# Sixteen weight tiles a layer split into high and low parts by two GpSimd DMAs instead of by ScalarE and VectorE

## The chip, the cores and the metric

The program runs on one core of a Trainium2 chip. The metric is the time of one execution on the device in microseconds, the median of several runs. The five engines of the core have their own instruction queues, each worked off in order: TensorE (PE, with its weight loads as PEld), VectorE (DVE), ScalarE (ACT), GpSimd (POOL) and SyncE (SP, which here only issues DMAs).

## The reference

Two layers act on `x` (512 positions, 1024 columns, float32). The part that matters here is the first third of each layer, the mixer:

```python
h = rms_norm(x, g_mix[l])
z = h @ w_in[l]                                  # 1024 -> 2560 columns
q, k, v, xb, gb = z[...]                         # 512 columns each
q = partial_rope(q, cos, sin); k = partial_rope(k, cos, sin)
o = diff_attention(q, k, v, lam)                 # 4 heads, two softmaxes each
c = centred_dwconv(xb, lru_conv_w[l], lru_conv_b[l])
h_f = rg_lru(c, ..., False); h_b = rg_lru(c, ..., True)   # sigmoid gates, exp, sqrt, scan
r = rms_norm((h_f + h_b) * jax.nn.gelu(gb), lru_norm_g[l])
x = x + jnp.concatenate([o, r], axis=-1) @ w_out[l]
```

After it come a cross-attention into 256 memory tokens and a squared-ReLU MLP, then the next layer, and a final norm.

## The kernel before

Every product is made of three TensorE passes in `float32r`: a float32 operand is split into a high part (rounded to float32r) and a low part (the rest), and the product is high by high, high by low and low by high. Activations are kept transposed, 128 rows of columns by 512 positions. Weights come from HBM as tiles of 128x1024 float32 (512 KB), 126 a layer (`NT`). Tile names in the profile: `wraw` is a weight tile as loaded, `whi` and `wlo` are its two parts, `b` are 62 buffers of 128x512, `mm` and `at` are PSUM banks, `pt` holds transposed probabilities, `s` small columns.

`weight(l, t)` delivers a tile. It takes a `wraw` buffer (3 exist), loads it from SP's queue, has ACT write `whi` and DVE write `wlo` (`split`), and the consumer `gemm_fm` uses it in 24 matmuls of 512 columns. `whi` and `wlo` have 3 buffers each (`NW`), so the buffers that tile number n takes are free only when PE has finished with tile n-3. The sixteen tiles from `T_FM` on are the columns of q and k (8 tiles, `qk_one`), of `xb` (4, `lru_conv`) and of `gb` (4, `lru_branch`), all of the mixer. The tiles of v (`T_V`), of the gates (`T_G`), and everything behind the mixer are not among them.

The program is recorded first and then ordered by a planner (`Plan`). Each recorded operation has a key, the PE time recorded so far less a lead (`plan.ahead`); `schedule` plays the engines through with cost estimates and always places the operation that can start first on its engine, the lowest key first. Loads of `wraw` lead by 65 (`LOAD_AHEAD`), splits by 12 (`SPLIT_AHEAD`). An activation whose function is not in the table that ACT holds is set back by `SWITCH`, since ACT must load a table first. Engines then run the emitted order, each in its own queue.

In the mixer, heads of attention (16 units of a score, softmax, transpose and value product) are mixed with filler pieces in the order of `ORDER`: conv tiles (X, Y), gates (P, R: 8 matmul groups each with a sigmoid on ACT, then exponentials, tanh), scans (p, r: square roots on ACT, scans on DVE), gelu tiles (B), q and k of the next heads (1, 2, 3), then the norm (N) and the memory's keys and values (K). The functions of sigmoid, exp, sqrt and gelu lie in different tables. The line of every row is L412 of the kernel before and L416 of the changed one: the loop in `emit` that issues all recorded calls.

Of the kernel before, what the change touches and what calls it, by code (L numbers as in the profile page):

```python
# [12 lines left out]
F32R = mybir.dt.float32r  # L13
I32 = mybir.dt.int32
AF = mybir.ActivationFunctionType
ALU = mybir.AluOpType
AX = mybir.AxisListType

P = 128
# [8 lines left out]
T_FM = 0  # L28
# [9 lines left out]
NT = 126  # L38
# [10 lines left out]
ATT_AHEAD = 3  # L49
SPLIT_AHEAD = 12.0  # L50
LOAD_AHEAD = 65.0


PC = {}
# [96 lines left out]
class Plan:  # L151
# [43 lines left out]
    def cost(self, eng, m, a, k):  # L195
        out = a[0] if a else k["out"]
        n = 1
        for d in out.shape[1:]:
            n *= d
        if eng == "pe":  # L200
            if m == "transpose":
                return 0.109
            f32 = a[1].root.dtype == F32
            if n < 64:
                return 0.224
            return n * 0.00176 if f32 else max(0.114, n * 0.000456)
        if m == "dma_start":
            return 0.06
        if eng == "act":
            t = 0.093 + n * 0.000833  # L210
            t += 0.093 * sum(isinstance(k.get(x), _View) for x in ("scale", "bias", "accum_out"))
            return t
        if eng == "dve":
            if m == "tensor_reduce":
                n = 512
            if m == "tensor_scalar_mul":
                return 0.066 + n * 0.0007
            ap = m == "scalar_tensor_tensor" and isinstance(a[2], _View)
            return 0.067 + n * 0.00105 + 0.06 * ap
        if eng == "pool":  # L220
            return 0.1 + n * (0.0022 if m != "memset" else 0.001)
        return 0.06

    def record(self, eng, m, a, k):
        allv = [v for v in (*a, *k.values()) if isinstance(v, _View)]
        out = [v for v in (a[0] if a else k["out"], k.get("accum_out")) if isinstance(v, _View)]
        op = self.cur
        if not isinstance(op, _Op):
            op = _Op()
            op.eng, op.calls, op.dur, op.idx = eng, [], 0.0, len(self.ops)  # L230
            op.succ, op.roots, op.new, op.ready, op.preds, op.behind = {}, [], [], 0.0, set(), set()
            op.table, op.bytes = None, 0
            op.key = self.t - self.lead
            self.ops.append(op)
            if self.cur == "open":
                self.cur = op
        assert op.eng == eng
        op.calls.append((m, a, k))
        c = self.cost(eng, m, a, k)
        op.dur += c  # L240
        if eng == "pe":
            self.t += c
        if m == "dma_start":
            v = out[0] if out else k["in_"]
            op.bytes = 4
            for d in v.shape:
                op.bytes *= d
        if m == "activation":
            op.table = self.SETS.get(str(a[2]).split(".")[-1])
        for v in allv:  # L250
            w = any(v is o for o in out)
            r, b = v.root, v.box
            if w and eng == "pe":
                b = [0, r.shape[0], 0, r.shape[1]]
            if r not in op.roots:
                op.roots.append(r)
                r.left += 1
                if not r.log:
                    op.new.append(r)
                    r.first = op  # L260
                else:
                    op.behind.add(r.first)
            for o, ob, ow in r.log:
                if o is not op and (w or ow) and b[0] < ob[1] and ob[0] < b[1] and b[2] < ob[3] and ob[2] < b[3]:
                    op.preds.add(o)
            if w and b[0] <= 0 and b[2] <= 0 and b[1] >= r.shape[0] and b[3] >= r.shape[1]:
                r.log = [e for e in r.log if e[0] is op]
            r.log.append((op, b, w))
# [146 lines left out]
def trunk(tc, ctx, xT, memT, pos, W, par, outT):  # L415
# [4 lines left out]
    plan = Plan(nc, {  # L420
        "const": (cst, 0),
        "b": (sb, NB), "xb": (sb, 2), "rb": (sb, 1), "Cr": (sb, 1), "Sr": (sb, 1),
        "wraw": (sb, NRAW), "whi": (sb, NW), "wlo": (sb, NW), "pt": (sb, 4), "s": (sb, NSM),
        "mm": (ps, NMM), "at": (ps, 8 - NMM),
    })
    V, A, G, PE, SP = (plan.engine(e) for e in ("dve", "act", "pool", "pe", "sp"))
# [19 lines left out]
    def b(v):  # L446
        return v.bitcast(F32)


    def split(dst_hi, dst_lo, src):  # L450
        A.activation(dst_hi, src, AF.Copy)
        V.tensor_tensor(dst_lo, src, b(dst_hi), op=ALU.subtract)
# [7 lines left out]
    def raw_weight(l, t, ahead=None):  # L460
        raw = plan.tile("wraw", [P, 1024], F32)
        if ahead:
            for h in range(2):
                cs = slice(h * 512, h * 512 + 512)
                with plan.ahead(ahead[h]):
                    SP.dma_start(out=raw[:, cs], in_=W[l * NT + t][:, cs])
        else:
            with plan.ahead(LOAD_AHEAD):
                SP.dma_start(out=raw, in_=W[l * NT + t])
        return raw  # L470

    def weight(l, t):
        raw = pre.pop(t, None) if l == 0 else None
        first = raw is not None
        if raw is None:
            raw = raw_weight(l, t)
        hi = plan.tile("whi", [P, 1024], F32R)
        lo = plan.tile("wlo", [P, 1024], F32R)
        with plan.ahead(SPLIT_AHEAD):
            for cs in (slice(0, 512), slice(512, 1024)) if first else (slice(0, 1024),):  # L480
                split(hi[:, cs], lo[:, cs], raw[:, cs])
        return hi, lo

    def gemm_fm(l, t, xs, out, order=range(KD)):

        hi, lo = weight(l, t)
        for i, k in enumerate(order):
            xh, xl = xs[k]
            wh = hi[:, k * P:(k + 1) * P]
            with plan.group():  # L490
                PE.matmul(out, wh, xh, start=(i == 0), stop=False)
                PE.matmul(out, wh, xl, start=False, stop=False)
                PE.matmul(out, lo[:, k * P:(k + 1) * P], xh, start=False, stop=(i == KD - 1))
# [182 lines left out]
    def v_products(l, xget):  # L676
        pms = [MM(), MM(), AT(), AT()]
        for t in range(4):
            hi, lo = weight(l, T_V + t)
            for k2 in range(2):  # L680
                k = 2 * t + k2
                xh, xl = xget(k)
                wh = hi[:, k2 * S:(k2 + 1) * S]
                wl = lo[:, k2 * S:(k2 + 1) * S]
                for c in range(4):
                    a_ = xh[:, c * P:(c + 1) * P]
                    with plan.group():
                        PE.matmul(pms[c], a_, wh, start=(k == 0), stop=False)
                        PE.matmul(pms[c], a_, wl, start=False, stop=False)
                        PE.matmul(pms[c], xl[:, c * P:(c + 1) * P], wh, start=False, stop=(k == 7))  # L690
        return pms
# [25 lines left out]
    def lru_gates(l, pr, conv, neg, posi):  # L717

        gh, gl = weight(l, T_G + pr)
        gs = {}  # L720
        for c2 in range(2):
# [311 lines left out]
    def mem_load():  # L1033
        out = []
        for i in range(2):
            m = plan.tile("wraw", [P, 1024], F32)
            with plan.ahead(LOAD_AHEAD):
                SP.dma_start(out=m, in_=memT[:, 1024 * i:1024 * (i + 1)])
# [404 lines left out]
```

## Time and profile before

| | |
|---|---|
| median of 3 runs | 1533.76 us (1530.17 to 1539.23) |
| the profiled execution's own time | 1536.88 us |
| its span | 1535.1 us |
| PE, PEld busy | 1476.1, 1242.4 us |
| DVE, ACT busy | 1183.5, 727.1 us |
| POOL busy | 54.1 us |
| TensorE's mean granted clock | 0.978 |

The span is the time between the first and last instruction of one execution. Busy time of an engine is not the time that it sets the pace; that is read from the waits.

### The profile page before, as it was taken

The page shows a single profiled execution, that of the slowest core. Times are in us where ns is not written, and L with a number is a line of the kernel's source. Part 1 is how long each engine was busy: PE and PEld are TensorE (multiplying, and loading weights), DVE is VectorE, ACT ScalarE, POOL GpSimd, SP SyncE. Part 2 cuts the span into 40 slices and gives each one's busy share as a digit, 9 for nine tenths or more (in the row PEclk, how much of TensorE's full clock was granted, in tenths as well). Part 3 has the DMA queues.
Part 4 walks back from the last instruction along what each step waited for, and adds up shares of the span by engine and source line. Part 5 has one row for each costly group of instructions (what it writes and reads, how often), then busy time and mean ns, then how long its engine had stood idle before and what let it go on. Part 6 is the DMA issues. An engine that isn't in the chain of part 4 may idle for free.

```text
span 1535.1 us, 20895 instructions
## 1 busy us (share of the span) xinstructions
PE 1476.1 (96%) x8038; PEld 1242.4 (81%) x8038; DVE 1183.5 (77%) x2107; ACT 727.1 (47%) x1099; POOL 54.1 (4%) x59
## 2 busy tenths in 40 slices
PE   8979999999999999999999799999999999999996
PEld 6757788888889889898977577888888898988985
DVE  7899886655589696979868876865656887969696
ACT  5587664444334343434535875553443433434243
POOL 0031000000000000000001310000000000000000
PEclk9989999999999999999999987999999999999998
DMA  5322342311222323222242213422112323232321
GB/s 194 97 82 78 129 138 82 110 69 56 96 96 83 110 84 122 98 97 97 87 134 81 85 57 110 144 101 96 55 69 82 110 84 107 86 110 83 116 88 58
DMA packets 45107, 148.24 MB, mean 97 GB/s; under 512 B 5584, under 2 KB 5712, under 8 KB 45008
## 3 DMA queue, kind: packets, MB, share of 16 engines
q1 hardware_dynamic: 44864, 146.65, 28.0%
q8 instruction: 63, 1.03, 0.3%
q14 instruction: 36, 0.29, 0.1%
q10 hardware_dynamic: 144, 0.26, 0.0%
HBM read 136.41 MB, written 2.10 MB: 90 GB/s over the span
## 4 chain that ended last, share of the span: by engine, by line
PE 85%; DVE 10%; issue 2%; DMA 1%; ACT 1%; SPq 0%; DVEq 0%; ACTq 0%
PE mm L412 65%; PE at L412 20%; DVE b L412 6%; DVE wlo L412 2%; DVE pt L412 1%; DVE s L412 1%; ACT b L412 1%; DMA b<-b 0%; DVE c_x L412 0%; DMA wraw<-in_W 0%; DMA c_x<-in_xT 0%; DMA wraw<-in_memT 0%; SPq L412 0%; ACT whi L412 0%; ACT Cr L412 0%
## 5 line engine op out<-in xcount | busy, mean ns | idle before, releaser
L412 PE MATMUL mm<-b,whi 128*128 128x512 f32 (+1 forms) x3648 | 991.3, 359 | 13.0 <-ACT b L412 6.2
L412 PEld LDWEIGHTS mm<-b,whi 128*128 128x128 f32 x3648 | 638.5, 190 | 126.3 <-ACT b L412 8.6
L412 PE MATMUL mm<-b,wlo 128*128 128x512 f32 (+1 forms) x1824 | 651.0, 357 | 8.0 <-DVE wlo L412 8.0
L412 ACT ACTIVATE whi<-wraw 128x1024 fp32r<-128x1024 f32 (+1 forms) x223 | 233.7, 1049 | 372.6 <-issue 168.3
L412 PEld LDWEIGHTS mm<-b,wlo 128*128 128x128 f32 x1824 | 345.8, 190 | 64.7 <-DVE wlo L412 10.0
L412 DVE TENSOR_TENSOR wlo<-wraw,whi 128x1024 fp32r<-128x1024 f32 (+1 forms) x223 | 277.1, 1243 | 37.2 <-ACT whi L412 36.9
L412 DVE TENSOR_TENSOR b<-b,b 128x512 fp32r<-128x512 f32 (+3 forms) x374 | 219.2, 602 | 15.6 <-ACT b L412 13.3
L412 ACT ACTIVATE b<-b 128x256 fp32r<-128x256 f32 (+2 forms) x224 | 130.3, 596 | 151.9 <-DVE b L412 151.3
L412 DVE TENSOR_TENSOR c_x<-c_x,mm 128x256 f32<-128x256 f32 (+1 forms) x160 | 73.8, 472 | 73.0 <-PE mm L412 71.6
L412 ACT ACTIVATE whi<-pt 128x1024 fp32r<-128x1024 f32 x64 | 67.9, 1061 | 101.6 <-PE mm L412 75.5
L412 PE MATMUL at<-b,whi 128*128 128x256 f32 x512 | 91.8, 278 | 0.0
L412 DVE TENSOR_TENSOR b<-mm,rb 128x512 f32<-128x512 f32 x72 | 49.5, 687 | 53.2 <-PE mm L412 52.5
L412 PE MATMUL at<-b,b 128*128 128x256 f32 (+1 forms) x320 | 83.9, 371 | 3.1 <-DVE b L412 2.2
L412 ACT ACTIVATE b<-at,s 128x512 f32<-128x512 f32 (+2 forms) x100 | 61.0, 614 | 41.9 <-DVE s L412 41.4
L412 DVE TENSOR_TENSOR wlo<-pt,whi 128x1024 fp32r<-128x1024 f32 x64 | 78.2, 1221 | 0.6 <-ACT whi L412 0.3
L412 DVE TENSOR_REDUCE s<-at 128x1 f32<-128x512 f32 (+1 forms) x80 | 54.4, 688 | 31.3 <-PE at L412 31.3
L412 PEld LDWEIGHTS at<-b,whi 128*128 128x128 f32 x512 | 77.6, 188 | 0.0
L412 PEld LDWEIGHTS at<-b,b 128*128 128x128 f32 x320 | 50.1, 195 | 30.9 <-issue 22.6
L412 PE MATMUL at<-b,wlo 128*128 128x256 f32 x256 | 71.1, 278 | 0.0
L412 PE MATMUL at<-pt,b 128*128 128x256 f32 (+1 forms) x288 | 53.1, 332 | 4.2 <-ACT pt L412 2.9
L412 PEld LDWEIGHTS at<-pt,b 128*128 128x128 f32 x288 | 45.3, 200 | 12.2 <-ACT pt L412 3.9
L412 DVE TENSOR_TENSOR c_x<-c_x,at 128x256 f32<-128x256 f32 x96 | 40.1, 419 | 18.1 <-PE at L412 17.7
(124 smaller groups left out, 1311.4 us busy)
## 6 DMA issues: line engine op xcount, KB each, us to landing
wraw<-in_W SPq DMA_DIRECT2D x249, 512.0 KB, 3.2
b<-b SPq DMA_DIRECT2D x64, 128.0 KB, 2.4
wraw<-in_memT SPq DMA_DIRECT2D x4, 512.0 KB, 3.9
out_T<-b SPq DMA_DIRECT2D x8, 256.0 KB, 2.6
c_x<-in_xT SPq DMA_DIRECT2D x7, 256.0 KB, 5.5
wraw<-in_W SPq DMA_DIRECT2D x6, 256.0 KB, 5.5
c_x<-in_xT ACTq DMA_DIRECT2D x1, 256.0 KB, 3.3
c_prm<-in_par SPq DMA_DIRECT2D x1, 89.0 KB, 3.2
```

The lines of the kernel that those rows point to most:

```text
L412: getattr(self.engines[op.eng], m)(*a, **k)
```

## The change

For the sixteen tiles from `T_FM` on, `weight` now calls `weight_dma`. It takes no `wraw`. A DMA issued from GpSimd's queue reads the tile from HBM and writes it, converted to float32r, to `whi`. ACT writes the negative of `whi` to `wlo`. A second DMA from GpSimd's queue reads the same weights from HBM again and adds them to `wlo`. The planner's cost of a DMA issued on GpSimd is raised to 1.1, and an accumulating DMA counts twice its bytes.

```diff
+CAST_AHEAD = 28.0
+NEG_AHEAD = 20.0
...
         if m == "dma_start":
-            return 0.06
+            return 1.1 if eng == "pool" else 0.06
...
+            if "accum_op" in k:
+                op.bytes *= 2
...
+    def weight_dma(l, t):
+
+        hi = plan.tile("whi", [P, 1024], F32R)
+        lo = plan.tile("wlo", [P, 1024], F32R)
+        src = W[l * NT + t]
+        with plan.ahead(CAST_AHEAD):
+            G.dma_start(out=hi, in_=src)
+        with plan.ahead(NEG_AHEAD):
+            A.activation(lo, b(hi), AF.Copy, scale=-1.0)
+            G.dma_start(out=lo, in_=src, accum_op=ALU.add)
+        return hi, lo
+
     def weight(l, t):
+        if T_FM <= t < T_FM + 16:
+            return weight_dma(l, t)
         raw = pre.pop(t, None) if l == 0 else None
```

The planner orders everything anew, so rows move on every engine. PE's order has the same 7580 rows in both; ACT's has 983 rows before and 999 now, and its ACT_TABLE_LOAD rows are 26 before and 43 now: 15 and 22 in the first layer, 11 and 21 in the second. DVE loses 32 subtractions, SP 32 loads, and GpSimd gains 64 DMAs.

On ACT, in the first layer, between the exponentials of the first gates and the sigmoids of the second gates, before (`b<-mm,c_prm` are sigmoids, `c_dneg` and `c_dpos` the decay scales of exp and tanh, `b<-b` alone a square root or a plain copy):

```order
L412 ACT_TABLE_LOAD
L412 ACTIVATE b_791<-b_791 128x512
L412 ACTIVATE b_835<-b_835 128x512
L412 ACTIVATE b_851<-b_851 128x512
L412 ACTIVATE b_869<-b_869 128x512
L412 ACTIVATE b_1047<-b_1028 128x512
L412 ACT_TABLE_LOAD
L412 ACTIVATE b_1050<-mm_994,c_prm_70 128x512
L412 ACTIVATE b_1061<-mm_1002,c_prm_70 128x512
L412 ACTIVATE b_1068<-mm_1035,c_prm_70 128x512
L412 ACTIVATE b_1076<-mm_1064,c_prm_70 128x512
L412 ACTIVATE b_1084<-mm_1072,c_prm_70 128x512
```

The four square roots stood together behind one table load, and the sigmoids behind the next. The same place now (`s` beside `at` marks a softmax exponential):

```order
L416 ACTIVATE wlo_1076<-whi_1056 128x1024
L416 ACT_TABLE_LOAD
L416 ACTIVATE b_1079,s_719<-at_876,s_900 128x512
L416 ACTIVATE b_984<-b_984,c_dpos_332 128x512
L416 ACT_TABLE_LOAD
L416 ACTIVATE b_1088<-mm_1052,c_prm_70 128x512
L416 ACTIVATE b_1100<-b_1086 128x512
L416 ACT_TABLE_LOAD
L416 ACTIVATE b_984<-b_984 128x512
L416 ACTIVATE pt_898<-at_1111 128x512
L416 ACTIVATE b_1147<-b_1122 128x512
L416 ACT_TABLE_LOAD
```

Three of the square roots have moved ahead of this piece, behind a load of their own; the fourth, a sigmoid, a softmax exponential and a tanh now follow each other with a table load between them, and a negation of a weight tile (`wlo<-whi`) stands among them.

On GpSimd, from the start of the first layer to the rope multiplications of the first head (`Sr` is the sine table), before:

```order
L412 MEMSET b_110 128x512
L412 TENSOR_TENSOR b_488<-b_488,Sr_504 128x512
L412 TENSOR_TENSOR b_548<-b_548,Sr_504 128x512
L412 MEMSET xb_650 128x2 x2
L412 MEMSET xb_737 128x2 x2
```

And now:

```order
L416 MEMSET b_110 128x512
L416 DMA whi_266<-in_W 128x1024
L416 DMA wlo_309<-in_W 128x1024
L416 DMA whi_352<-in_W 128x1024
L416 DMA whi_417<-in_W 128x1024
L416 DMA wlo_419<-in_W 128x1024
L416 DMA wlo_478<-in_W 128x1024
L416 DMA whi_529<-in_W 128x1024
L416 TENSOR_TENSOR b_533<-b_533,Sr_531 128x512
L416 DMA wlo_576<-in_W 128x1024
L416 DMA whi_604<-in_W 128x1024
L416 TENSOR_TENSOR b_597<-b_597,Sr_531 128x512
```

The two multiplications that make q and k of the first head stand behind seven and nine DMAs of their queue, each of which waits there for a buffer or for ACT's negation.

## Rows read from the trace of the kernel before

**Rows 1.** The page: the span, and TensorE's granted clock in 40 slices, tenths.

```profile
span 1535.1 us, 20895 instructions
PEclk9989999999999999999999987999999999999998
```

**Rows 2.** The page: the chain that ended last, by engine.

```profile
PE 85%; DVE 10%; issue 2%; DMA 1%; ACT 1%; SPq 0%; DVEq 0%; ACTq 0%
```

**Rows 3.** Busy times by stretch: PE, PEld, DVE, ACT, POOL, clock, DMA share, GB/s.

```profile
20.00:200.00 180.00, 168.47 (x775) 130.60 (x774) 157.05 (x338) 120.60 (x196) 25.63 (x24) 0.94 0.31 100
60.00:130.00 70.00, 59.61 (x237) 43.49 (x236) 61.22 (x99) 57.95 (x93) 17.13 (x16) 0.88 0.21 68
780.00:960.00 180.00, 163.98 (x722) 126.15 (x721) 142.69 (x268) 113.16 (x182) 24.09 (x20) 0.91 0.29 92
840.00:900.00 60.00, 47.45 (x188) 33.30 (x187) 46.59 (x85) 53.76 (x89) 16.60 (x11) 0.86 0.24 73
200.00:780.00 580.00, 573.77 (x3285) 494.60 (x3284) 439.59 (x739) 241.97 (x353) 0.00 (x0) 1.00 0.27 95
```

**Rows 4.** PE's waits from 20 to 200 us: us in total, times, longest.

```profile
PE mm L412 <- ACT b L412: 3.9, 2, 3.4
PE mm L412 <- DVE b L412: 3.0, 1, 3.0
PE at L412 <- DVE b L412: 2.2, 1, 2.2
PE at L412 <- ACT b L412: 1.3, 1, 1.3
PE at L412 <- DVE pt L412: 0.6, 1, 0.6
```

**Rows 5.** PE's waits from 780 to 960 us.

```profile
PE at L412 <- ACT b L412: 9.8, 1, 9.8
PE at L412 <- ACT pt L412: 2.9, 1, 2.9
PE mm L412 <- ACT b L412: 2.3, 3, 1.3
PE at L412 <- DVE pt L412: 0.5, 2, 0.3
```

**Rows 6.** PE's waits for low parts, whole span.

```profile
PE mm L412 <- DVE wlo L412: 8.0, 9, 1.3
```

**Rows 7.** Groups by shape: busy us, mean ns of one | idle before.

```profile
L412 DVE TENSOR_TENSOR wlo<-wraw,whi 128x1024 fp32r<-128x1024 f32 x217 | 273.0, 1258 | 36.5 <-ACT whi L412 36.2
...
L412 ACT ACTIVATE whi<-wraw 128x1024 fp32r<-128x1024 f32 x217 | 230.0, 1061 | 371.3 <-issue 168.3 <-PE mm L412 148.3 <-PE at L412 37.1
...
L412 ACT ACT_TABLE_LOAD x26 | 33.4, 1283 | 1.6 <-PEq L1435 1.2
...
L412 POOL TENSOR_TENSOR b<-b,Sr 128x512 f32<-128x512 f32 x16 | 22.4, 1398 | 768.3 <-ACT Sr L412 647.5 <-DVE b L412 94.2 <-ACT whi L412 26.6
```

**Rows 8.** The page: DMA issues, KB each, us from issue to landing.

```profile
wraw<-in_W SPq DMA_DIRECT2D x249, 512.0 KB, 3.2
...
wraw<-in_W SPq DMA_DIRECT2D x6, 256.0 KB, 5.5
```

**Rows 9.** PE's timeline: start us, us, instruction; 39 to 48 us.

```profile
39.48 0.60 PE L412 MATMUL at<-c_ident,b 128*128 128x128 f32 x4
39.84 0.72 PE L412 MATMUL mm<-b,whi 128*128 128x512 f32 x2
...
41.76 0.63 PE L412 MATMUL mm<-b,whi 128*128 128x512 f32 x2
...
47.36 0.63 PE L412 MATMUL mm<-b,whi 128*128 128x512 f32 x2
```

## The prediction

> **What bounds the kernel now.** The page's chain of waits comes first: 85% of it is PE and 10% DVE [rows 2], so time is lost only where PE waits or where its clock is low. The clock by slices dips in the third slice and in the 24th and 25th, besides the last [rows 1]; these are the mixers of the two layers, where the sixteen tiles are used. The busy times by stretch say the same: from 200 to 780 us PE is busy 573.77 of 580 us at clock 1.00, whereas it idles 11.5 us of the first mixer's 180 and 16.0 us of the second's [rows 3]. Inside them two stretches are worst: 60 to 130 us (PE idle 10.4 us, clock 0.88) and 840 to 900 us (12.6 us, 0.86) [rows 3]; the gates and scans lie there. PE's waits by releaser show who ends them: of 11.0 us in the first mixer 5.8 end with DVE and 5.2 with ACT [rows 4]; of 15.5 us in the second, 15.0 with ACT and 0.5 with DVE [rows 5]. ACT is busy 57.95 of 70 us in the first bad stretch and 53.76 of 60 in the second [rows 3], although over a whole mixer only about two thirds. So DVE and ACT share the blame in layer one, and ACT has nearly all of it in layer two.
>
> **What is removed.** 32 subtractions of 1.258 us leave DVE [rows 7]: 40.3 us of busy time. What that is worth on the path is bounded by waits that DVE ends. PE waited for a low part 8.0 us in the whole run [rows 6], but no such wait stands among the waits of the two mixers [rows 4, 5], so nothing of it belongs to these tiles. The other waits for DVE in the mixers sum to 3.0 + 2.2 + 0.6 + 0.5 = 6.3 us [rows 4, 5]. A gain is at least 0 and at most those 6.3 us (with the clock that they cost, below, 11). I take half, -3.2 us, since a wait for DVE in the first mixer stands beside one for ACT, which would come next. SP's 32 loads vanish at no gain: no PE wait in either mixer ends with a weight load [rows 4, 5]. The 32 conversions on ACT are replaced by 32 negations of the same shape and output type, 1.06 us each [rows 7]: 0.
>
> **What is added: two DMAs in a chain.** Before, a tile's parts were ready one ACT and one DVE instruction (2.3 us) after buffers came free, since the raw tile waited in its own buffer. Now nothing can start before `whi` is free, and then come issue, landing, negation, issue, landing. The trace has neither a GpSimd-issued nor an accumulating DMA. From below: a landing of 3.2 us for 512 KB [rows 8], the negation, and a second landing of 3.2: 7.5 us. From above: an issue on GpSimd as long as its 1.40 us multiplication [rows 7], a landing of 5.5 as in the crowded start [rows 8], a table load of 1.28 ahead of the negation, the negation, another issue, and 5.5 twice for a DMA that reads both addends: 21.6 us. I take 1.40 + 3.2 + 1.06 + 1.40 + 2 x 3.2 = 13.5 us: loads beyond the start landed in 3.2, and two operands must be read.
>
> Against this stands the room: PE's work between the last matmul of the tile that frees the buffers and the first low-part matmul of the new one. Eight weight rows of three matmuls take 47.36 - 41.76 = 5.6 us, so 0.233 us a matmul of 512 columns, half for 256, and four transposes 0.36 us [rows 9]. Two tiles lie between, 2 x 5.6 = 11.2 us, plus two matmuls of its own, 11.7; the attention in between is counted from the changed order. The rooms are, in layer one, 12.1, 13.1, 13.1, 12.1, 14.9, 14.9, 15.6, 15.2, 16.0, 16.0, 11.9, 11.9, 13.6, 17.1, 15.4 and 12.7 us; in layer two 12.0, 13.1, 13.1, 11.9, 14.7, 14.7, 14.1, 13.2, 15.3, 14.5, 16.6, 15.2, 14.5, 14.2, 14.1 and 13.2. A stall at one tile also lengthens the room of the next two. So at 13.5 us layer one stalls 1.4 (first q tile) + 1.4 (second conv tile) + 1.6 (first gelu tile) + 0.8 (last k tile) = 5.2 us, layer two 1.5 + 1.6 + 0.3 + 0.3 = 3.7: together **+8.9 us**. By the same recurrence a chain of 12 us costs nothing, 16 us 32, 18 us 54, 21.6 us 97.
>
> The Trainium skill ("DMA: Bandwidth & Descriptors", section on the anatomy of a DMA on the gpsimd path) gives 2.0 us plus bytes over 436 GB/s, an estimate of 3.2 us for such a tile; this case's hardware-queue loads agree with 3.2, no run here shows the gpsimd path yet. Its "Collectives: The Full Stack" (section on the bandwidth ceiling) says an adding DMA is slower for its two source reads and not for the add. With both, the second landing would be 4.4 us, the chain 8.7, and the term 0.
>
> **What is moved: ACT's order.** The table loads go from 26 to 43, the seventeen new ones among gates, scans and gelus, at 1.283 us [rows 7]: 21.8 us more ACT work. Nothing is gained by it; it costs nothing if ACT's idle time takes it. That idle time is 12.0 us in 60 to 130 and 6.2 in 840 to 900 [rows 3], mostly too scattered. Bounds 0 and 21.8; I take two thirds, **+14.5 us**, near the upper end because ACT ends the longest waits there. Behind each load stand sigmoids, whose results free the three product banks, and softmax exponentials, for which PE's transposes wait.
>
> **What is added: a wait at the head of ACT's queue.** A negation waits for a landing, and exponentials behind it wait too. Bounds: 0, and 32 x (5.5 - 3.2) = 74 us if every landing is as late as in the crowded start. I count the eleven negations that stand among gates and scans in the changed order, each held by one GpSimd issue, 1.40 us, half of it on the path: **+7.7 us**. On GpSimd the rope and gate multiplications stand behind DMAs that wait for that same negation; they hide behind tiles already queued on PE and get nothing of their own unless the landing is late (a rival).
>
> **The clock.** In the two bad stretches 0.12 x 70 = 8.4 and 0.14 x 60 = 8.4 us of clock went with 10.4 and 12.6 us of idleness [rows 3], so 0.7 to 0.8 us for one. Short chain stalls are spread out; to the table term I add half: **+7.2 us**.
>
> Sum: -3.2 + 14.5 + 8.9 + 7.7 + 7.2 = +35.1 us. The profiled execution took 1536.88 us, 1.8 beyond its span of 1535.1, and would become 1572.0; it lies 3.1 us above the median of the runs, so I forecast 1533.8 + 35.1 = **1569 us**. About 0.5% (7.7 us) is what a measurement of this kernel can tell from no change.
>
> **The rivals.**
> Only the table loads cost: the chain stays under 12 us and landings come before their negations. -3.2 + 14.5 + 7.2 = +18.5, 1552 us. For it: DMA engines are busy a third at most in the mixers [rows 3]. Against: 256 KB loads took 5.5 us when several queued [rows 8]. The skill's two sentences lead here.
> A long chain: the accumulating DMA takes much longer than two loads. 18 to 21.6 us cost 54 to 97 instead of 8.9, 1614 to 1657 us. For it: no row shows what an add costs. Against: idle DMA engines.
> ACT held at its head: half of the 74 us counts instead of 7.7, +64, 1598 us. For it: ACT is the last releaser in layer two; against: over a whole mixer it is idle a third.
> No change: table loads fall into ACT's idle time, the chain hides, and DVE's relief pays what remains: 1534 us.
> Faster: DVE is what holds the scans from 60 to 130 us, where it is busy 61.22 of 70 us [rows 3]. Free of its subtractions for these tiles there, it feeds products and scores sooner; all 6.3 us of waits go, with 0.75 of clock each, -11, 1523 us. It decides only if the chain is under 11.9 us, the smallest room, and ACT's extra loads are hidden.
>
> **How the numbers follow.** Forecast 0.42 (its own range 1552 to 1592), table loads alone 0.18, long chain 0.15, ACT held 0.07, no change 0.10, faster 0.08. The range from 1530 to 1630 leaves out the faster case and the longer half of the long chain, with some of what lies at its ends. Faster by over 0.5%: 0.07; within 0.5%: 0.13, the case of no change and the lucky end of the table loads; slower: 0.80, the rest.
>
> **What would show it.** The DVE group `wlo<-wraw,whi` at 185 instructions of 1024 columns; 43 table loads near 1.28 us; landings in the DMA issues of GpSimd near 4.6 us from issue for `whi` and 7.8 for `wlo`; PE waits ended by DMA `wlo` of 1 to 2 us at the first q and second conv tile; ACT negations waiting for DMA `whi`; lower clock in the same slices; nothing moved from 300 to 700 us but a later start. The prediction is wrong if landings are far longer, if ACT absorbs its loads, or if PE's waits in the mixers shrink.

## The result and the profile after

The changed kernel took 1555.14 us, median of 4 runs (1553.62 to 1559.57), beside 1532.16 us for the kernel before (4 runs): a ratio of 1.0146, 95% interval 1.0106 to 1.0187. The forecast was 1569 us, slower. It is slower by 23 us, for other reasons than most of those forecast, as is shown below. The profiled execution is the slowest of the four.

The profiled execution after took 1559.57 us, its span 1557.6. The page: span and TensorE's granted clock in 40 slices, then the chain that ended last by engine.

```profile
span 1557.6 us, 20956 instructions
PEclk9897999999999999999999979999999999999998
PE 82%; DVE 8%; ACT 4%; DMA 3%; issue 2%; POOL 1%; SPq 0%; DVEq 0%; POOLq 0%; ACTq 0%
```

Against [rows 1, 2], ACT has grown from 1% to 4% of the chain and DMA from 1% to 3%, GpSimd has come into it, and in the first mixer the low clock has gone from the third slice to the second and fourth. PE's busy time is 1483.9 us, so PE idled 73.7 us of the span where it idled 59.0 before: 14.7 us more, and the 7.8 us by which the same 8038 matmuls took longer go with the lower clock. Together they are the 22.5 us by which the span grew.

PE's waits by releaser, from 20 to 200 us (first block) and from 780 to 960 us (second block): us in total, times, longest.

```profile
PE mm L416 <- DVE b L416: 10.5, 2, 10.2
PE at L416 <- DMA b<-b: 4.9, 2, 3.7
PE mm L416 <- DMA wlo<-in_W: 3.2, 2, 2.1
PE at L416 <- ACT rb L416: 3.0, 1, 3.0
...
PE mm L416 <- ACT b L416: 5.6, 3, 2.5
PE mm L416 <- DVE b L416: 4.3, 2, 2.4
PE at L416 <- ACT b L416: 3.0, 2, 2.5
PE at L416 <- DMA b<-b: 3.0, 1, 3.0
PE mm L416 <- DMA wlo<-in_W: 0.9, 1, 0.9
```

In the first mixer [rows 4] had no wait over 3.4 us; now there is one of 10.2. In the second the wait of 9.8 us of [rows 5] is gone, and shorter ones stand in its place. Copies `b<-b` end 7.9 us of waits in the two mixers, where they ended 0.8 in the kernel before, and landing low parts end 4.1 us that did not exist.

The DMA issues of the page: KB each, median us from issue to landing.

```profile
whi<-in_W POOLq DMA_DIRECT2D x32, 512.0 KB, 4.4
wlo<-in_W POOLq DMA_DIRECT2D x32, 512.0 KB, 5.2
b<-b SPq DMA_DIRECT2D x64, 128.0 KB, 2.8
```

Groups by shape: busy us, mean ns of one | idle before, and what ended it.

```profile
L416 DVE TENSOR_TENSOR wlo<-wraw,whi 128x1024 fp32r<-128x1024 f32 x185 | 228.1, 1234 | 25.8 <-ACT whi L416 25.7
L416 ACT ACT_TABLE_LOAD x43 | 55.2, 1283 | 2.7 <-PEq L1453 1.2 <-DVE b L416 0.8
L416 ACT ACTIVATE wlo<-whi 128x1024 fp32r<-128x1024 f32 x32 | 33.7, 1053 | 31.9 <-DMA whi<-in_W 27.3 <-DVE s L416 3.6 <-issue 1.1
L416 POOL DMA_DIRECT2D wlo<-in_W x32 | 28.3, 883 | 103.3 <-ACT wlo L416 103.1 <-issue 0.2
L416 POOL DMA_DIRECT2D whi<-in_W x32 | 20.3, 636 | 667.5 <-PE at L416 594.9 <-PE mm L416 55.3 <-DVE b L416 17.1
```

The subtractions and table loads are as many as forecast. The converting DMA lands in 4.4 us, the adding one in 5.2, and ACT stood 27.3 us with a negation at the head of its queue that waited for a landing.

### The profile page after: what moved, and what is told of

The parts are those of the page before. It is cut to its first block, busy times and chain, and to the rows that moved or that the text cites. A ratio compares the mean times of both kernels' runs of the same rounds, so it can differ in the third digit from the quotient of the medians.

```text
span 1557.6 us, 20956 instructions
## 1 busy us (share of the span) xinstructions
PE 1483.9 (95%) x8038; PEld 1242.8 (80%) x8038; DVE 1144.8 (73%) x2075; ACT 750.3 (48%) x1116; POOL 95.4 (6%) x123
## 4 chain that ended last, share of the span: by engine, by line
PE 82%; DVE 8%; ACT 4%; DMA 3%; issue 2%; POOL 1%; SPq 0%; DVEq 0%; POOLq 0%; ACTq 0%
PE mm L416 63%; PE at L416 19%; DVE b L416 5%; ACT b L416 2%; DMA whi<-in_W 2%; DVE wlo L416 2%; DMA b<-b 1%; DVE pt L416 1%; ACT L416 1%; DVE s L416 1%; POOL b L416 0%; DMA wlo<-in_W 0%; ACT wlo L416 0%; DVE c_x L416 0%; DMA c_x<-in_xT 0%
## 5 line engine op out<-in xcount | busy, mean ns | idle before, releaser
L416 PE MATMUL mm<-b,whi 128*128 128x512 f32 (+1 forms) x3648 | 994.6, 361 | 25.8 <-DVE b L416 14.7
L416 ACT ACTIVATE whi<-wraw 128x1024 fp32r<-128x1024 f32 (+1 forms) x191 | 199.8, 1046 | 313.1 <-issue 143.3
L416 DVE TENSOR_TENSOR wlo<-wraw,whi 128x1024 fp32r<-128x1024 f32 (+1 forms) x191 | 232.3, 1216 | 26.0 <-ACT whi L416 25.9
L416 DVE TENSOR_TENSOR b<-b,b 128x512 fp32r<-128x512 f32 (+3 forms) x374 | 217.7, 596 | 28.9 <-ACT b L416 21.2
L416 POOL DMA_DIRECT2D whi<-in_W x32 | 20.3, 636 | 667.5 <-PE at L416 594.9
L416 ACT ACT_TABLE_LOAD x43 | 55.2, 1283 | 2.7 <-PEq L1453 1.2
```

The lines of the kernel that those rows point to most:

```text
L416: getattr(self.engines[op.eng], m)(*a, **k)
```

## The experiments

Beside the change twelve kernels, each with its ratio to the kernel before on the same chip (95% interval) and, for reading, what that ratio makes of 1534 us. Four of them leave work out or compute other values (without the adding DMA, second DMA overwrites, order of the change, no subtractions), and so do the two with one table load; they are there to price a part.

| kernel | median us (before) | ratio | us |
|---|---|---|---|
| the change | 1555.14 (1532.16) | 1.0146 (1.0106 to 1.0187) | +22 |
| without the adding DMA | 1542.17 (1535.36) | 1.0051 (1.0033 to 1.0070) | +8 |
| second DMA overwrites | 1548.11 (1534.16) | 1.0097 (1.0068 to 1.0127) | +15 |
| order of the change, work of before but its loads | 1546.76 (1535.36) | 1.0085 (1.0068 to 1.0101) | +13 |
| before, planned with 44 table loads | 1547.32 (1535.36) | 1.0088 (1.0067 to 1.0108) | +13 |
| the change, planned with 28 table loads | 1560.17 (1535.36) | 1.0168 (1.0146 to 1.0189) | +26 |
| the change with one table load | 1553.86 (1534.16) | 1.0135 (1.0110 to 1.0161) | +21 |
| before with one table load | 1535.30 (1534.16) | 1.0011 (0.9992 to 1.0029) | +2 |
| converting DMA alone, planned anew | 1546.35 (1534.16) | 1.0086 (1.0060 to 1.0111) | +13 |
| order of before, both DMAs | 1583.87 (1535.10) | 1.0319 (1.0288 to 1.0350) | +49 |
| order of before, converting DMA alone | 1578.97 (1535.10) | 1.0293 (1.0266 to 1.0321) | +45 |
| order of before, no subtractions | 1520.98 (1535.10) | 0.9905 (0.9881 to 0.9928) | -15 |
| order of before, GpSimd subtracts | 1566.38 (1531.44) | 1.0229 (1.0203 to 1.0256) | +35 |

**Table loads.** Two theories stood against each other: the table loads and ACT's new order cost most (as the prediction had it), or the chain of DMAs and the queues that it holds. First the planner's price for a change of table was altered.

In the kernel before:

```diff
-    SWITCH = 25.0
+    SWITCH = 0.0
```

In the changed kernel:

```diff
-    WAIT = 2.5
+    WAIT = 1.0
...
-                        st += self.WAIT if st > free_at[e] else 0.0
+                        st += self.WAIT
```

> The kernel before, all its work as it was, but the planner no longer sets back an activation that needs another table: 44 table loads in place of 26, in an order of its own. Table theory (a table load in the mixers costs two thirds of its 1.28 us and half of that again in clock): 18 x 1.28 x 2/3 x 1.5 = 23 us more than before, 1550 to 1557 us. Chain theory (table loads fall into ACT's idle time): within 6 us of before, 1530 to 1538 us.

> The changed kernel with all its DMAs and negations, but planned so that an activation that needs another table always pays a wait of 1.0: 28 table loads in place of 43, and an order of its own. Table theory: most of the loss goes, 1535 to 1541 us. Chain theory: the chain of DMAs is as long as before, so 1550 to 1557 us.

The kernel before became 13 us slower with 44 loads, not 23; the changed one did not become faster with 28. The number of loads does not rank these four times (26, 28, 43 and 44 loads: 1535, 1560, 1555 and 1547 us), but both kernels also have an order of their own. So the loads were taken out at a fixed order:

```diff
+                if m == "activation" and str(a[2]).split(".")[-1] in self.SETS:
+                    a = a[:2] + [AF.Tanh] + a[3:]
                 getattr(self.engines[op.eng], m)(*a, **k)
```

> The changed kernel in its own order, but every function that needs a table (exp, sigmoid, square root, gelu, sine) is replaced by tanh, so that 43 table loads become one; the values computed are then others. To be read against the same replacement in the kernel before. Table theory, at two thirds of 1.28 us and half of that again in clock: the 17 additional loads cost 22 us, so this kernel and its counterpart differ by under 5 us. Chain and order theory (loads fall into ACT's idle time; the adding DMA and the places of rows make the loss): they differ by 15 us or more. Half and half, as the order alone at 11 us and the adding DMA at 13 us suggest: they differ by 10 to 15 us.

> The kernel before with the same replacement: every function that needs a table becomes tanh, 26 table loads become one. Table theory at the same price per load: 26 x 1.28 x 2/3 x 1.5 = 33 us less than before, about 1500 us. Chain and order theory: the loads stand in idle time for the most part, 1522 us or more.

ACT_TABLE_LOAD by shape, of the changed kernel with tanh alone:

```profile
L418 ACT ACT_TABLE_LOAD x1 | 1.3, 1283 | 1.2 <-PEq L1455 1.2
```

42 loads, 53.9 us of ACT work, are gone, and 21 of 22 us of the loss are still there; in the kernel before 25 loads (32.1 us) are worth nothing. The difference between the two is 19 us instead of 22, and these 3 us lie within the intervals, which leave some 8 us either way. So the table theory, which put 22 us on the 17 loads, has fallen. It does not follow that every load is free. Window from 100 to 140 us and PE's longest wait in it, of the changed kernel with tanh alone:

```profile
100.00:140.00 40.00, 29.22 (x81) 18.81 (x80) 24.07 (x35) 21.09 (x37) 11.63 (x11) 0.66 0.35 79
PE mm L418 <- ACT b L418: 6.5, 1, 6.5
```

The wait of 10.2 us is 6.5 here, and PE is busy 29.22 us of the 40 (second number) instead of 23.50, but at a clock of 0.66 instead of 0.73. Over the whole profiled executions PE idles 66.5 us instead of 73.7. The times of the runs show next to nothing of this (1554 and 1555 us).

The Trainium skill ("ScalarE: Activation LUTs", section on what ACT_TABLE_LOAD costs) gives 1283 ns for a load, as these rows do; what of it PE pays no single row tells.

**The adding DMA.** Both kernels keep the changed order row by row.

The first leaves the adding DMA out, the second lets it overwrite:

```diff
-                getattr(self.engines[op.eng], m)(*a, **k)
+                if "accum_op" not in k:
+                    getattr(self.engines[op.eng], m)(*a, **k)
```

```diff
+                k.pop("accum_op", None)
                 getattr(self.engines[op.eng], m)(*a, **k)
```

> The changed kernel in its own order, without the adding DMA: the converting DMA and the negation stay, the low part is left as the negative of the high part (so the addition of the weights is left out). Table theory (the 17 additional table loads and ACT's new order make most of the 23 us): only PE's 4.1 us of waits for a landing low part and the clock that goes with them can come back, so 1548 to 1553 us. Chain theory (the second landing, GpSimd's queue behind it and the traffic that slows the SBUF copies make it): about 1540 us or less.

> The changed kernel in its own order, the second DMA still behind the negation but overwriting in place of adding (so the low part becomes a second copy of the high part, and the sum is left out). If the adding itself costs (two source reads, a landing of 5.2 us), this comes to the 1542 us of the kernel without the second DMA, and its landings are under 4.6 us. If any second DMA in the chain costs (its issue on GpSimd, its place ahead of the next converting DMA in the queue), 1550 to 1557 us.

Without it 14.6 us of 22 come back, far more than PE's 4.2 us of waits for it. About half goes with any second DMA (+15 against +8) and half with its adding (+22 against +15); by the intervals the first half is 7 us, 5 either way, and the second 7.5 us, 8 either way, so that its size is not quite told from nothing. So the first answer is that of the chain theory within 2 us, and the second lies between the two that were expected. Rows of the overwriting kernel and of the one without, median landing last:

```profile
whi<-in_W POOLq DMA_DIRECT2D x32, 512.0 KB, 4.5
wlo<-in_W POOLq DMA_DIRECT2D x32, 512.0 KB, 3.8
```

```profile
whi<-in_W POOLq DMA_DIRECT2D x32, 512.0 KB, 3.7
b<-b SPq DMA_DIRECT2D x64, 128.0 KB, 2.3
```

An overwriting second DMA lands in 3.8 us, an adding one in 5.2; and in this order the converting one lands later with a second DMA on the queue, in 4.4 or 4.5 us instead of 3.7. A second DMA is not the only thing that does this: the converting DMA alone, planned anew (below), also lands in 4.5. Where this matters is seen once near the start. Timeline of the changed kernel, GpSimd, ACT and PE together (start us, us, instruction, idle before and its releaser):

```profile
26.49 0.88 POOL L416 DMA_DIRECT2D wlo<-in_W  x1 [6.24 <-ACT wlo L416]
27.07 0.88 POOL L416 DMA_DIRECT2D whi<-in_W  x1
...
33.77 1.06 ACT L416 ACTIVATE wlo<-whi 128x1024 fp32r<-128x1024 f32 x1 [4.76 <-DMA whi<-in_W]
...
39.39 0.58 ACT L416 ACTIVATE rb<-at 128x512 f32<-128x512 f32 x1
...
40.03 1.79 PE L416 MATMUL at<-c_ident,b 128*128 128x128 f32 x8 [2.98 <-ACT rb L416]
```

The same place without the adding DMA:

```profile
25.74 0.54 POOL L417 DMA_DIRECT2D whi<-in_W  x1 [4.76 <-PE at L417]
...
29.45 1.06 ACT L417 ACTIVATE wlo<-whi 128x1024 fp32r<-128x1024 f32 x1 [0.45 <-DVE c_rtmp L417]
...
36.65 0.58 ACT L417 ACTIVATE rb<-at 128x512 f32<-128x512 f32 x1
```

With the adding DMA issued 0.58 us ahead of it on GpSimd, the next tile's negation starts 6.7 us after the issue, and ACT has stood for 4.76 us of that; without, it starts 3.7 us after the issue. `rb`, the norm's scale, is behind it in ACT's queue and 2.7 us later, and PE waits 2.98 us. Then the clock follows. Windows from 20 to 80 us and from 100 to 140 us of four kernels (length, PE, PEld, DVE, ACT, POOL busy, clock, DMA share, GB/s), first the kernel before:

```profile
20.00:80.00 60.00, 59.52 (x259) 45.24 (x258) 50.02 (x133) 31.79 (x49) 4.99 (x10) 1.00 0.32 106
100.00:140.00 40.00, 32.61 (x114) 23.25 (x115) 35.56 (x61) 31.58 (x52) 9.01 (x5) 0.79 0.22 71
```

the changed order with the work of before (the next experiment):

```profile
20.00:80.00 60.00, 58.26 (x255) 43.81 (x253) 55.96 (x162) 34.12 (x62) 2.99 (x8) 1.00 0.18 53
100.00:140.00 40.00, 24.93 (x76) 16.68 (x77) 22.73 (x34) 26.84 (x40) 7.70 (x6) 0.70 0.12 27
```

the change without the adding DMA:

```profile
20.00:80.00 60.00, 58.46 (x250) 44.50 (x249) 47.36 (x152) 33.47 (x59) 7.57 (x16) 0.97 0.43 123
100.00:140.00 40.00, 24.92 (x72) 16.55 (x73) 21.90 (x35) 27.48 (x40) 8.51 (x7) 0.70 0.19 51
```

and the change:

```profile
20.00:80.00 60.00, 54.76 (x209) 40.58 (x208) 39.60 (x138) 27.94 (x51) 11.89 (x19) 0.89 0.66 158
100.00:140.00 40.00, 23.50 (x74) 15.19 (x73) 22.86 (x37) 29.09 (x44) 8.50 (x9) 0.73 0.40 92
```

From 20 to 80 us the change idles 3.7 us more than the kernel without the adding DMA and loses 0.08 x 60 = 4.8 us of clock: 8.5 us in this one stretch. The two profiled executions are further apart than the medians, 21.2 us (spans 1557.6 and 1536.4); PE's 3000th matmul, between the mixers, starts 8.4 us later with the adding DMA (619.7 and 611.3 us), so layer one's part lies in this stretch, and the other 13 us in the second mixer.

**The order.** In the second of these windows three kernels with the changed order look alike, whatever DMAs they have. The one with the work of before was made so:

```diff
+                if op.eng == "pool" and m == "dma_start" and "accum_op" not in k:
+                    continue
+                if k.get("scale") == -1.0 and op.roots[0] in self.hi_of:
...
+                    self.engines["act"].activation(hi.tile.rearrange("p (a c) -> p a c", c=P), one, AF.Copy)
+                elif "accum_op" in k:
...
+                    self.engines["dve"].tensor_tensor(k["out"].rearrange("p (a c) -> p a c", c=P), one, hi, op=ALU.subtract)
```

> The order of the changed kernel with the work of the kernel before: for the sixteen tiles neither DMA is issued, ACT writes the high part by a plain copy where it negated, DVE writes the low part by a subtraction where the adding DMA stood. The weights of these tiles are left out: both instructions read a resident tile of ones. So 43 table loads and ACT's new order are in, the DMAs, their waits and their traffic are out, and DVE has its 32 subtractions again. Table theory: 1548 to 1556 us. Chain theory: 1530 to 1538 us.

It came 13 us above before, between the two expectations. (It also lacks the 32 loads of the raw tiles, but no wait of PE in the mixers ended with one of these [rows 4, 5].) From 100 to 140 us it idles 7.7 us more than before and loses 0.09 x 40 = 3.6 us of clock, 11.3 us together. By PE's 3000th matmul it is 16 us behind before (613.1 and 596.9 us), and in the second mixer it makes up 7 of these: the spans of the profiled executions are 9 us apart. So the new order is worse in layer one and better in layer two. PE's waits from 100 to 140 us:

```profile
PE mm L429 <- DVE b L429: 11.7, 2, 11.4
PE at L429 <- DMA b<-b: 3.7, 1, 3.7
```

Both are in the changed kernel too (10.2 and 3.7 us), so neither the wait for DVE nor that copy is a matter of the weights' DMAs: they come with the new places of the rows. The timeline shows which rows. DVE and PE of the kernel with the work of before:

```profile
98.93 0.72 DVE L429 STREAM_SHUFFLE b<-mm 128x512 f32<-128x512 f32 x1
...
101.64 1.23 DVE L429 TENSOR_TENSOR_SCAN b<-b,b 128x512 f32<-128x512 f32 x1
...
105.11 2.33 DVE L429 TENSOR_TENSOR_SCAN b<-b,b 128x512 f32<-128x512 f32 x2
...
107.94 0.68 DVE L429 TENSOR_TENSOR b<-mm,Cr 128x512 f32<-128x512 f32 x1
108.68 1.22 PE L429 MATMUL mm<-b,whi 128*128 128x512 f32 x2 [11.36 <-DVE b L429]
```

PE goes on right behind the second of the two rope rows that read a product bank (the shuffle, then the product with the cosine table `Cr`), and three scans with their products stand between the two. The product starts 9.0 us after the shuffle here and 7.9 in the changed kernel; in the kernel before it starts 4.05 us after it at most, in all sixteen places. Whether this row alone makes the wait was not tried.

**The DMAs in the order of before.** The other corner: the order of before, and in it the DMAs. Here `seq` holds the tiles in the order in which they take buffers.

```diff
+            i = max(last[seq["whi"][n - 3]], prev)
...
+            add.append((i, n, 0, ("cast", hi, src)))
...
+                q = max(bisect.bisect_left(start, start[i] + 5.5), i + 1, last[seq["wlo"][j - 3]] + 1, self.lo_at + 1)
...
+                add.append((q, n, 1, ("neg", hi, lo)))
+                add.append((q, n, 2, ("add", lo, src)))
```

> The work of the changed kernel in the order of the kernel before, with its 26 table loads: each converting DMA is put in as soon as PE's last use of the tile three earlier is past in that order, the negation and the adding DMA some 5.5 us of planned time behind it; the subtractions and raw loads of the sixteen tiles fall out, every other row keeps its place. Order theory (the new order makes half of the loss or more, the DMAs little): 1530 to 1542 us. Chain theory (the adding DMA, its landing and the negation at the head of ACT's queue make it): 1545 us or more.

> The kernel before in its own order, only that the high parts of the sixteen tiles come from converting DMAs put in as above in place of ACT's conversions; raw loads and DVE's subtractions stay. If the order made the loss of the half change (1546 us in its own order): 1528 to 1536 us. If GpSimd's DMAs cost by themselves: 1540 us or more.

Beside them, the converting DMA alone in the change's own manner, planned anew:

```diff
+        raw = raw_weight(l, t)
...
-            A.activation(lo, b(hi), AF.Copy, scale=-1.0)
-            G.dma_start(out=lo, in_=src, accum_op=ALU.add)
+            V.tensor_tensor(lo, raw, b(hi), op=ALU.subtract)
```

> Half of the change: the high part comes from the converting DMA, the raw tile is loaded as before and DVE subtracts as before; no negation, no adding DMA, ACT has 32 conversions less, 28 table loads in an order of its own. If the adding DMA and the negation that waits in ACT's queue make the loss: 1526 to 1536 us. If GpSimd's DMAs or their waits for buffers in its queue cost by themselves: 1540 us or more.

The two in the order of before are far slower, 49 and 45 us. That is on the side of the theories that blame the DMAs ("1545 us or more", "1540 us or more"), but neither expectation had a loss of this size. The places of the DMAs in this order are mine, and a better hand might save some of it. The groups that wait for the converting DMA, of the kernel with both DMAs and of that with the converting one alone, where DVE's subtraction takes the negation's part:

```profile
L452 ACT ACTIVATE wlo<-whi 128x1024 fp32r<-128x1024 f32 x32 | 33.8, 1057 | 104.4 <-DMA whi<-in_W 59.6
```

```profile
L461 DVE TENSOR_TENSOR wlo<-wraw,whi 128x1024 fp32r<-128x1024 f32 (+1 forms) x223 | 272.6, 1223 | 78.8 <-DMA whi<-in_W 39.3
```

Whichever engine reads the landed tile stands for it at the head of its queue: ACT 59.6 us, against 27.3 in the changed kernel, or DVE 39.3 us. SBUF copies `b<-b` land in a median of 4.2 and 4.3 us there, 2.8 in the changed kernel. So the new order is not a mere mishap beside the DMAs: it costs 13 us with the old work, and with the new work it is 27 us better than the old order with the DMAs in these places. The converting DMA alone in an order planned for it costs 13 us as well.

**DVE's relief.** The order of before, the subtraction first left out and then given to GpSimd:

```diff
+            if op.eng == "dve" and op.new and op.new[0] in self.skip:
+                op.new[0].tile = self.skip[op.new[0]].tile
+                continue
```

```diff
+                eng = "pool" if op.eng == "dve" and op.new and op.new[0] in self.relieved else op.eng
+                getattr(self.engines[eng], m)(*a, **k)
```

> The kernel before in its own order, without DVE's 32 subtractions of the sixteen tiles; the low passes read the high part again, so the low parts are left out. Relief theory (DVE's work is what PE waits for in the first mixer): 1523 to 1530 us. If DVE's waits are for ACT's results and not for its own time: within 3 us of before.

> The kernel before in its own order, with all its work, only that GpSimd in place of DVE makes the 32 subtractions of the sixteen tiles; no DMA is added. GpSimd's multiplication of 128x512 took 1.40 us, so a subtraction of 128x1024 is put at 2.8 us, 1.5 longer than DVE's and far under the room of 12 us. If DVE's relief is what the change was worth (14 us without the subtractions), most of it comes here: 1519 to 1528 us. If the rope and gate multiplications that then queue behind subtractions on GpSimd take it back, or both engines slow each other: 1532 to 1545 us.

Without the subtractions 15 us are gained, 5.2 us of PE's idle time (59.0 to 53.8) and 9.2 us of its busy time with the clock. Most of it lies in the second mixer, where the clock is 0.96 and was 0.91 [rows 3]:

```profile
780.00:960.00 180.00, 165.99 (x821) 129.84 (x820) 138.15 (x273) 120.82 (x196) 22.95 (x20) 0.96 0.34 102
```

PE's 3000th matmul starts 3.6 us earlier than before (593.3 and 596.9 us), its last one 14.4. With GpSimd subtracting, nothing of it is left, and the kernel is 35 us slower than before. DVE's products of two SBUF tiles, first without the subtractions, then with GpSimd subtracting, and GpSimd's group:

```profile
L416 DVE TENSOR_TENSOR b<-b,b 128x512 f32<-128x512 f32 x103 | 72.4, 711 | 11.9 <-POOL b L416 7.2 <-ACT b L416 4.4
```

```profile
L414 DVE TENSOR_TENSOR b<-b,b 128x512 f32<-128x512 f32 x103 | 97.3, 954 | 9.5 <-POOL b L414 7.1 <-ACT b L414 2.1
...
L414 POOL TENSOR_TENSOR wlo<-wraw,whi 128x1024 fp32r<-128x1024 f32 x32 | 81.1, 2537 | 675.1 <-ACT whi L414 650.8 <-ACT s L414 18.1 <-DMA wraw<-in_W 3.0
```

The same 103 products take 0.95 us instead of 0.71, and DVE's busy time, with the same 2075 instructions, is 1195.5 us instead of 1143.9: DVE took 52 us longer with GpSimd's 81 us of subtractions beside it, 25 of these in the 103 products. The Trainium skill ("GPSIMD Engine Reference", section Specifications) says that GpSimd shares its SBUF interface with VectorE and contends with instructions that have two SBUF inputs; these rows agree. GpSimd's DMA instructions do nothing of the kind: DVE's busy time in the changed kernel is 1144.8 us. How much of the 35 us comes from this, and how much from rows that now queue behind the subtractions on GpSimd, was not tried. No version that does all the work beats the kernel before.

## Why the prediction was right, and where its reasons were wrong

The sign and the range held, but the sum came within 14 us of the time with some luck: its errors cancel. By its own terms:

- **DVE's relief, -3.2 us**: mis-sized. In the order of before the relief is worth 15 us. The 5.2 us of idle time in it are under the bound of 6.3 that the waits gave, but that is partly luck: 11 of the 14.4 us between the profiled executions came in layer two, where [rows 5] had 0.5 us of waits for DVE. So waits that one engine ends do not bound what its relief is worth. What was too low is above all the clock that comes back, 9.2 us of busy time, 1.8 us for one of idle time where at most 0.75 was put.
- **Table loads, +14.5, with +7.2 of clock: this step failed.** At a fixed order the loads are worth 3 us, nothing within the intervals, and not 21.7. What went with them, the new places of the rows, costs 13 us with the work of before. The money was there, the cause was not: the new order was priced by its loads, and not by what now waits for what, such as PE for a rope row behind three scans.
- **Chain of DMAs, +8.9**: the mechanism was there, small. The adding DMA lands in 5.2 us and not in the 7.8 of the sum's chain (1.40 and two times 3.2); 4.4 + 1.06 + 5.2 = 10.7 us is under the smallest room of 11.9, and PE waited 4.2 us for low parts in all. The Trainium skill's two sentences would have given 4.4 us for this landing and no stall.
- **Negation at the head of ACT's queue, +7.7**: right in kind, too small. ACT held 27.3 us. How much of that PE pays was not taken out by itself; the adding DMA, which lets the next tile land later, costs 14.6 us as a whole, and in the profiled executions 8.5 us lie in the stretch of the hold that ends at 33.77 us.
- **The clock** fell in the stretches where PE's waits were, also from 20 to 80 us (1.00 to 0.89), which the prediction did not name.

A sum can be made to close: order +13, relief -15, adding DMA +15, and +9 for the converting DMA and its negation make 22. The last is what is left over: the step from the order alone to the change without the adding DMA is 13 to 8, and it is +9 only if the relief is worth as much in this order as in that of before, which was not tried.

Of the rivals, "only the table loads" gave 1552 us and was nearest to the time, with a cause that is now refuted. "Faster" named a true force, which the DMAs take back. Of what was to show it, the counts, the landing near 4.6 us for `whi` (4.4), the waits of 1 to 2 us for low parts (1.1, 2.1, 0.9) and the unchanged stretch from 200 to 780 us (573.75 us busy, as [rows 3]) came; the landing of 7.8 us did not. What stays open is why the order of before takes the DMAs so badly, how much the holds on ACT cost by themselves, and whether the rope row behind the scans makes the wait of 10.2 us alone.

## What to carry to other kernels

A transfer that can start only when its buffer comes free has little slack, and the engine that reads it holds what stands behind it in its queue, 27.3 us of ACT here: count the holds, not only the waits of the engine that sets the end. A count of instructions on an engine with idle time, such as the table loads here, is no price until they are taken out at a fixed order. And when a change makes a planner order everything anew, run the new order with the old work and the old order with the new: here they cost 13 and 49 us, and the change 22. Look at each layer too: the same order lost 16 us in one and won 7 in the other.

## What was not expected of the hardware

An adding DMA of 512 KB from GpSimd landed in 5.2 us and took 0.88 us of GpSimd; the same transfer overwriting took 3.8 and 0.55. A converting one into `whi` landed in 3.7 us without second DMAs and in 4.4 or 4.5 with them, in one order; in other orders it took 3.8 to 6.1. With 32 subtractions on GpSimd, 2.5 us each, DVE's work took 52 us longer.
